# Seven gate columns of the input projection moved next to and into the scan's prologue turns, with the modulation rows and their products in a new fixed order

## The chip, the cores and the metric

The kernel runs on one core of a Trainium2 chip, as one launch. The metric is the device time of that launch in microseconds, lower is better. The names of the engines in the profile are PE (matrix products), DVE (vector), ACT (scalar, activations), POOL (GpSimd) and SP (which here only issues DMAs); PEld is PE's weight load. Everything is fp32: where an operand needs more than one PE pass carries, it is split into a high and a low half (`hh`, `hl` for tokens; `whi`, `wlo` for weights), and a product is three matmuls.

## The reference, cut to what matters

One layer of a diffusion backbone, with 256 context tokens and 2048 latent tokens of width 1024.

```python
mod_x = silu(c) @ w_ada + b_ada                  # six vectors of 1024: sh1, sc1, ga1, sh2, sc2, ga2
mod_c = silu(c_ctx) @ w_ada + b_ada              # the same for the context; sh and sc are used
hx = rmsnorm(x, norm1_g) * (1 + sc1) + sh1
px = hx @ w_in                                   # 15 x 128 RWKV columns | 512 Fourier | 2 x 1024 gates
qx = rwkv_inputs(centred_shift(px[..., :1920]))  # r, decays, keys, values, ...; the same for ctx
yx = bidir_wkv(qx, states left by the context)   # two recurrent scans over the tokens
fx = real(fftn(px[..., 1920:2432]))              # over the 32 x 64 grid and the group channels
x = x + ga1 * ((sigmoid(gate_f) * (fx @ w_up_f)
                + sigmoid(gate_r) * (group_norm(yx) * g @ w_up_r)) @ w_out)
x = x + ga2 * swiglu(rmsnorm(x, norm2_g) * (1 + sc2) + sh2)
```

## The kernel before

*Prologue.* The rows of `w_ada` come in tiles `wadar` (128 x 1024) and are multiplied on DVE with the broadcast silu vectors, `sB` of the latents (`mod_dve`, L130) and `sC` of the context (L151); the sum over the row is accumulated into `mod`. Eight tiles give sc1 for both; sh1 comes from eight tiles `wadak` on PE into `modps` (L157). The statistics of the norm are in `rs`. Then every 256 tokens `xs` go through `scaled` (L249: x times gain times rs), `moved` on ACT (L253: plus shift, rounded, `hh`) and on DVE (L254: the rest, `hl`), for each of the eight k slices of 128 channels.

*Input projection.* Three parts of 768 tokens (part 0 holds the context and 512 latents). Each part runs fifteen column turns. A turn loads one RWKV column of `w_in`, multiplies it (`pxps`), shifts and post-processes it (`z_stage`, `stack_z`, `k_norm`; `bnps` is the last matmul of a z stage, its result goes by `bsq` into DRAM `bv_dr`), and then does one or two of the twenty Fourier and gate columns, 15 to 34 (`gate_columns`, PSUM tile `fps`): a column of 768 tokens is 24 matmuls of 512 and 24 of 256 tokens. Parts 1 and 2 also load one `wada` row tile in a turn (32 in all, two in the last) for the modulation that later stages need, each with one product on DVE; all use one buffer. These stages are ordered by a list scheduler, except the instructions that are marked `keep_in_program_order`.

*Scan.* From L568 on everything is pinned: each engine executes in the order of the program (in the profile all such instructions have the line of the helper, L568). The scan has 18 blocks of 128 tokens in both directions, in turns s = -2 to 17. Turns -2 and -1 are the prologue turns, which prepare the blocks 0 and 1: `gram` (PE, `qk` from the loaded `BD` and `KR`), `masks` (DVE, `QK`), a store and reload (`AI`), `invert` (DVE, `tm` and `Q`), a store and reload (`TT`, `T`), `wps`, `t21ps`. A turn from 0 on has two chains in addition, which end in the state `ZC`: PE `xr`, `pu`, `pz`, ACT copies, DVE `ZC`. Between the steps stand seven calls of `fill()` in a turn, each of which takes one step of the generator `fourier()`: first the DFT over the grid (`hps` and `p`), then the product with `w_up_f` (stored to `fm_dr`), then the group norm of the first four token blocks (`gny`, `gnb`, `sg`, `s`). Before, 140 of its 141 steps are taken in the twenty turns.

*After the scan.* `c_merge` multiplies the normed blocks with `w_up_r` (`pr`), adds the gated Fourier part (`gr`, `gf`), `c_out` multiplies with `w_out`; then the feed-forward layer to the end.

Of the kernel before, what the change touches and what calls it, by code (L numbers as in the profile page):

```python
# [40 lines left out]
def layer_kernel(ctx: ExitStack, tc, I, out_T, dbg=None):  # L41
# [44 lines left out]
    pcT = pcs.enter_context(tc.tile_pool(name="pcp", bufs=1, side="right")).tile([128, TOT // C, 2, 4], F32, name="pcT", padded_shape=[128, 40, 2, 4])  # L86
    hpx = ctx.enter_context(ExitStack())
# [17 lines left out]
    def stats(xs, bank, eng=nc.vector, n=256):  # L105
        rs = hp.tile([128, 256], F32, tag="rs", name="rs", bufs=4)[:, 0:n]
        sq = hp.tile([128, KT, 256], F32, tag="sq", name="sq", bufs=1)[:, :, 0:n]
        nc.scalar.activation(out=sq, in_=xs, func=AF.Square)
        for m in (4, 2, 1):
            eng.tensor_tensor(out=sq[:, 0:m, :], in0=sq[:, 0:m, :], in1=sq[:, m:2 * m, :], op=ALU.add)  # L110
        ps = bank()[:, 0:n]
        nc.tensor.matmul(ps, ones, sq[:, 0, :], start=True, stop=True)
        rms_finish(rs, ps)
        return rs
# [12 lines left out]
    RS = [stats(xs, mm_bank, nc.gpsimd) for xs in XS]  # L127

    def mod_dve(w, s_, jt, j):
        nc.vector.scalar_tensor_tensor(out=w, in0=w, scalar=0.5, in1=s_, op0=ALU.mult, op1=ALU.mult, accum_out=mod[:, jt, j:j + 1])  # L130

    with tc.tile_pool(name="wa", bufs=1) as wa:
        th = wa.tile([128, 16], F32, name="th")
        nc.scalar.activation(out=th, in_=vec[:, V_C:V_C + 16], func=AF.Tanh, scale=0.5)
        sc2 = wa.tile([128, 16], F32, name="sc2")
        nc.vector.scalar_tensor_tensor(out=sc2, in0=th, scalar=1.0, in1=vec[:, V_C:V_C + 16], op0=ALU.add, op1=ALU.mult)
        sc3 = wa.tile([128, 8, 2], F32, name="sc3")
        nc.vector.tensor_scalar(out=sc3.rearrange("p k j -> p j k"), in0=sc2.rearrange("p (j k) -> p j k", j=2),
                                scalar1=0.5, scalar2=None, op0=ALU.mult)
        sC = wa.tile([128, D], F32, name="sC")  # L140
        nc.sync.dma_start(sC, I["cc"][1:2, :].to_broadcast([128, D]))
        tB = wa.tile([128, D], F32, name="tB")
# [3 lines left out]
        mps = pmm.tile([128, 512], F32, tag="mm", name="modps")  # L146
        for n in range(8):
            wr = wa.tile([128, D], F32, tag="wr", name=f"wadar{n}", bufs=3)
            nc.sync.dma_start(wr, I["w_ada"][8 + n])
            wj = wa.tile([128, D], F32, tag="wj", name=f"wadaj{n}", bufs=1)  # L150
            nc.vector.scalar_tensor_tensor(out=wj, in0=wr, scalar=0.5, in1=sC, op0=ALU.mult, op1=ALU.mult,  # L151
                                           accum_out=mod[:, 8 + n, 1:2])
            mod_dve(wr, sB, 8 + n, 0)
            wk = wa.tile([128, KT, 128], F32, tag="wk", name=f"wadak{n}", bufs=3)
            nc.sync.dma_start(wk, I["w_ada0"][n])
            for k in range(KT):
                nc.tensor.matmul(mps[:, 2 * n:2 * n + 2], wk[:, k, :], sc3[:, k, :], start=k == 0, stop=k == KT - 1)  # L157
# [3 lines left out]
        nc.vector.tensor_copy(mod[:, 0:8, :], mps[:, 0:16].rearrange("p (j c) -> p j c", c=2))
# [70 lines left out]


    carry = cst.tile([128, 15, 1], F32, name="carry")

    with ExitStack() as st:
# [9 lines left out]

        def scaled(k, xs, rs, j):
            x_ = xs[:, k, :]
            nc.vector.scalar_tensor_tensor(out=x_, in0=x_, scalar=gsc[:, k, j:j + 1], in1=rs, op0=ALU.mult, op1=ALU.mult)  # L249

        def moved(k, xs, j, hh, hl):
            x_ = xs[:, k, :]
            nc.scalar.activation(out=hh[:, k, :], in_=x_, func=AF.Identity, bias=mod[:, k, j:j + 1])  # L253
            nc.vector.scalar_tensor_tensor(out=hl[:, k, :], in0=x_, scalar=mod[:, k, j:j + 1], in1=hh[:, k, :].bitcast(F32),  # L254
                                           op0=ALU.add, op1=ALU.subtract)
# [131 lines left out]

        NP = 3
        for part in range(NP):
# [3 lines left out]
            cols = [(512, 256), (258, 0)] if part == 0 else [(512, p0), (258 if part < 2 else 256, p0 + 512)]  # L393
            H = [[hp.tile([128, KT, 512 - 248 * i], F32R, tag=f"h{y}{i}", name=f"h{y}{part}_{i}")[:, :, 0:n] for y in "hl"]
                 for i, (n, _) in enumerate(cols)]

            places = [(0, 0, 0), (0, 256, 0), (1, 0, 1 if part == 0 else 0)]
            for ps_ in (places[0:2], places[2:3]):
# [21 lines left out]
            for ci, ct in enumerate((12, 13, 0, 8, 4, 1, 9, 5, 2, 10, 6, 3, 11, 7, 14)):  # L420
                if part:
                    for jt in range(16 * part + ci, 16 * part + ci + 1 + (ci == 14)):
                        wr = hp.tile([128, D], F32, tag="sq", name=f"wada{jt}", bufs=1, padded_shape=[128, 2 * D])
                        tc.keep_in_program_order(nc.sync.dma_start(wr, I["w_ada"][jt]))
                        mod_dve(wr, sB, jt, 0)
# [54 lines left out]
                gate_columns((15 + ci, 30 + ci // 3) if ci % 3 == 2 else (15 + ci,), H, lats)  # L480
# [81 lines left out]
    class Pinned:  # L562
        def __init__(self, eng):
            self.eng = eng

        def __getattr__(self, name):
            f = getattr(self.eng, name)
            return lambda *a, **k: tc.keep_in_program_order(f(*a, **k))  # L568

    PE, DV, AC, GP, SY = [Pinned(x) for x in (nc.tensor, nc.vector, nc.scalar, nc.gpsimd, nc.sync)]  # L570

    with ExitStack() as st:
# [5 lines left out]

        ZC = sp.tile([128, 2, 4, 64], F32, name="ZC")
# [230 lines left out]
        def fourier():  # L810
            with tc.tile_pool(name="fd", bufs=1) as fd:
# [602 lines left out]
```

## Time and profile before

| | us |
|---|---|
| median of 3 runs | 3577.69 (3574.19 to 3580.49) |
| the profiled execution | 3574.86 |
| its span in the trace | 3573.1 |
| prologue to the first token matmul | 0 to 60 |
| input projection, three parts | 60 to 1053 |
| from its last matmul to the first of the scan | 1053 to 1066 |
| prologue turns | 1066 to 1135 |
| scan | 1135 to 1813 |
| to the first `pr` | 1813 to 1826 |
| merge, output, feed-forward | 1826 to 3573 |

The mean granted clock of PE is 0.952 of full speed, PE is busy in 91% of the span, DVE in 67%. In the rows of waits the figures are the total, the number of times, and the longest; a name behind `<-` in square brackets is what ended the idle time before the instruction. Rows of groups read: busy us, mean ns of one, idle time of the engine just before them.

### The profile page before, as it was taken

The numbers are of one execution on the slowest core, as the hardware profiler recorded it, in microseconds if no ns is written. First come the engines' busy times: TensorE is split into PE (matmuls) and PEld (weight loads), VectorE is DVE, ScalarE is ACT, GpSimd is POOL, SyncE is SP. The second block draws the span as 40 slices with busy tenths as digits, with TensorE's granted clock in tenths as the row PEclk, the third lists the DMA queues.
The fourth block names the chain that finished last, engine by engine and source line by source line (L and its number), as shares of the span: only waits on it lengthen the run. The fifth ranks groups of instructions, "written<-read, shape, count | busy, mean of one in ns | idle before, by whom it ended". The sixth has DMA issues, their size and how long they took to land.

```text
span 3573.1 us, 56290 instructions
## 1 busy us (share of the span) xinstructions
PE 3265.4 (91%) x20574; PEld 2696.8 (75%) x20574; DVE 2408.0 (67%) x4466; ACT 1553.2 (43%) x2908; POOL 697.1 (20%) x1099
## 2 busy tenths in 40 slices
PE   5999899999987888889769997999999999999987
PEld 5887788877875777777657776888877878888876
DVE  6577577746757776666568678777774387776354
ACT  3668557646643444344434235333353333333332
POOL 2142332222323332122132341000120000000000
PEclk9999999999997888999779999999999999999998
DMA  6254554545455567767467764222264332222442
GB/s 221 88 172 154 173 188 150 173 148 183 167 191 155 139 173 218 219 192 218 140 241 235 251 229 145 92 82 84 83 203 168 130 108 86 80 84 94 158 166 101
DMA packets 308436, 561.01 MB, mean 157 GB/s; under 512 B 91296, under 2 KB 102816, under 8 KB 308160
## 3 DMA queue, kind: packets, MB, share of 16 engines
q1 hardware_dynamic: 264256, 418.29, 36.1%
q0 software_dynamic: 43904, 139.12, 11.9%
q8 instruction: 163, 2.67, 0.3%
q14 instruction: 113, 0.93, 0.1%
HBM read 405.62 MB, written 151.66 MB: 156 GB/s over the span
## 4 chain that ended last, share of the span: by engine, by line
PE 28%; issue 12%; DVE 6%; DMA 3%; ACT 1%; POOL 1%; SPq 0%; DVEq 0%; POOLq 0%; ACTq 0%
PE pd L1267 12%; PE pT L199 2%; PE pT L200 2%; PE pT L201 2%; PE pB L199 2%; PE pB L200 2%; PE pB L201 2%; PE po L201 1%; PE po L199 1%; PE po L200 1%; DMA gr<-g_dr 1%; DVE wlo L193 1%; DMA wraw<-w_down 1%; DMA wA<-w_gu 1%; POOL u_dr L1215 1%
## 5 line engine op out<-in xcount | busy, mean ns | idle before, releaser
L193 DVE TENSOR_TENSOR wlo<-wraw,whi 128x512 fp32r<-128x512 f32 x472 | 318.5, 698 | 416.5 <-ACT whi L192 393.7
L192 ACT ACTIVATE whi<-wraw 128x512 fp32r<-128x512 f32 x472 | 283.3, 626 | 481.1 <-PE pd L1267 200.3
L1267 PE MATMUL pd<-uh,whi 128*128 128x512 f32 x704 | 278.5, 396 | 25.0 <-ACT whi L192 23.4
L199 PE MATMUL fps<-hh,whi 128*128 128x512 f32 (+1 forms) x800 | 285.9, 357 | 0.1
L201 PE MATMUL fps<-hh,wlo 128*128 128x512 f32 (+1 forms) x800 | 281.7, 352 | 0.1
L200 PE MATMUL fps<-hl,whi 128*128 128x512 f32 (+1 forms) x800 | 280.0, 350 | 0.0
L1267 PE MATMUL pd<-ul,whi 128*128 128x512 f32 x704 | 277.4, 394 | 0.0
L1267 PE MATMUL pd<-uh,wlo 128*128 128x512 f32 x704 | 254.6, 392 | 0.6 <-DVE wlo L193 0.6
L199 PE MATMUL pxps<-hh,whi 128*128 128x512 f32 (+2 forms) x720 | 248.8, 346 | 5.8 <-ACT hh L253 3.5
L200 PE MATMUL pxps<-hl,whi 128*128 128x512 f32 (+2 forms) x720 | 244.4, 341 | 4.7 <-DVE hl L254 4.7
L201 PE MATMUL pxps<-hh,wlo 128*128 128x512 f32 (+2 forms) x720 | 242.6, 342 | 0.5 <-DVE wlo L193 0.4
L1205 DVE TENSOR_TENSOR u<-u,pT 128x512 f32<-128x512 f32 x176 | 120.7, 686 | 142.6 <-PE pT L201 140.9
L1215 POOL DMA_DIRECT2D u_dr<-u x44 | 23.8, 541 | 842.3 <-DVE u L1214 811.1
L1267 PEld LDWEIGHTS pd<-uh,whi 128*128 128x128 f32 x704 | 134.1, 191 | 58.2 <-ACT whi L192 27.1
L568 DVE TENSOR_TENSOR tm<-Q,AI 128x126 f32<-128x126 f32 (+22 forms) x558 | 149.0, 267 | 42.9 <-DMA AI<-ab_dr 26.5
L199 PEld LDWEIGHTS fps<-hh,whi 128*128 128x128 f32 x800 | 150.8, 188 | 25.6 <-issue 4.3
L200 PEld LDWEIGHTS fps<-hl,whi 128*128 128x128 f32 x800 | 150.7, 188 | 24.2 <-issue 5.5
L201 PEld LDWEIGHTS fps<-hh,wlo 128*128 128x128 f32 x800 | 150.5, 188 | 23.4 <-issue 2.4
L568 DVE TENSOR_TENSOR Q<-Q,tm 128x126 f32<-128x126 f32 (+22 forms) x558 | 154.4, 277 | 20.2
L199 PEld LDWEIGHTS pxps<-hh,whi 128*128 128x128 f32 x720 | 136.5, 190 | 25.9 <-ACT hh L253 4.3
L1267 PEld LDWEIGHTS pd<-ul,whi 128*128 128x128 f32 x704 | 134.1, 191 | 27.9
L1267 PEld LDWEIGHTS pd<-uh,wlo 128*128 128x128 f32 x704 | 133.1, 189 | 29.2 <-DVE wlo L193 1.4
(715 smaller groups left out, 8550.3 us busy)
## 6 DMA issues: line engine op xcount, KB each, us to landing
wraw<-w_in SPq DMA_DIRECT2D x210, 256.0 KB, 3.1
wraw<-w_down SPq DMA_DIRECT2D x176, 256.0 KB, 2.9
wA<-w_gu SPq DMA_DIRECT2D x176, 256.0 KB, 2.6
BD<-bd_dr SPq DMA_DIRECT2D x36, 512.0 KB, 7.1
KR<-kr_dr SPq DMA_DIRECT2D x36, 512.0 KB, 8.1
wada<-w_ada SPq DMA_DIRECT2D x32, 512.0 KB, 4.5
wraw<-w_out SPq DMA_DIRECT2D x64, 256.0 KB, 3.2
wf<-wf_dr SPq DMA_DIRECT2D x32, 512.0 KB, 7.0
```

The source lines that it names most:

```text
L192: nc.scalar.activation(out=hi[:, k0:k1, :], in_=raw, func=AF.Copy)
L193: nc.vector.tensor_tensor(out=lo[:, k0:k1, :], in0=raw, in1=hi[:, k0:k1, :].bitcast(F32), op=ALU.subtract)
L199: nc.tensor.matmul(ps, wh[:, k, :], xh(k), start=start and k == 0, stop=False)
L200: nc.tensor.matmul(ps, wh[:, k, :], xl(k), start=False, stop=False)
L201: nc.tensor.matmul(ps, wl[:, k, :], xh(k), start=False, stop=stop and k == K - 1)
L568: return lambda *a, **k: tc.keep_in_program_order(f(*a, **k))
L1205: nc.vector.tensor_tensor(out=o, in0=x, in1=y, op=ALU.add)
L1215: nc.gpsimd.dma_start(u_dr[f][:, TT[hf]:TT[hf] + 512], c)
L1267: nc.tensor.matmul(PD[ct], x[:, ct, :], y, start=f == 0 and i == 0, stop=f == FT - 1 and i == 2)
```

## The change

Four things move.

1. *Prologue.* The products of the modulation, PE's `modps` matmuls, the ends of the statistics and the scaling of the first 512 latents are pinned, in this order: for each tile its `sB` product, and for the first five also its `sC` product; then per k slice and 256 tokens `xs`, `hh`, `hl`; the `sC` products of the last three tiles stand behind slices 3, 5 and 7.
2. *Modulation rows.* All 32 `wada` tiles are loaded in part 1, two or three in a turn, none in part 2.
3. *Gate columns.* Part 2 does only the columns 15 to 25 within its turns (RWKV column 7 comes last instead of 14), then 26 and 27, and then a new generator `late_gates()` does 28 to 34: nine of its steps (columns 28 to 30, tile `gps`) before the scan, the other twelve (31 to 34) in the fourteen `fill()` calls of turns -2 and -1. `fourier()` starts with turn 0. It has one step more than before, one extra call, and 127 calls within the scan; its last fifteen steps are taken behind the last turn.
4. *Memory.* The token halves live in a pool of their own until turn 0; then that room holds one of the three `QK` tags and one of the two `TT`. The tile `fo` of the gate columns has two buffers instead of three. The last addition of the statistics has its own tile `sm`.

```diff
+    hst = ctx.enter_context(ExitStack())
+    hh_ = hst.enter_context(tc.tile_pool(name="hh", bufs=1))
...
-            nc.vector.scalar_tensor_tensor(out=wj, in0=wr, scalar=0.5, in1=sC, op0=ALU.mult, op1=ALU.mult,
-                                           accum_out=mod[:, 8 + n, 1:2])
-            mod_dve(wr, sB, 8 + n, 0)
+            WR.append(wr)
+            w0 = wa.tile([128, D], F32, tag="w0", name=f"wada0{n}", bufs=1)
+            DV.scalar_tensor_tensor(out=w0, in0=wr, scalar=0.5, in1=sB, op0=ALU.mult, op1=ALU.mult, accum_out=mod[:, 8 + n, 0:1])
+            if n < 5:
+                mod_j1(n)
...
-                nc.tensor.matmul(mps[:, 2 * n:2 * n + 2], wk[:, k, :], sc3[:, k, :], start=k == 0, stop=k == KT - 1)
+                PE.matmul(mps[:, 2 * n:2 * n + 2], wk[:, k, :], sc3[:, k, :], start=k == 0, stop=k == KT - 1)
+            if n in (3, 6):
+                RS[n // 3 - 1] = RS[n // 3 - 1](PE, DV)
...
+        scale_of(0)
+        for k in range(KT):
+            for m in range(2):
+                scaled(k, XS[m], RS[m], 0, DV)
+                moved(k, XS[m], 0, *[x[:, :, 256 * m:256 * m + 256] for x in H0[0]], DV)
+            if k in (3, 5, 7):
+                mod_j1(5 + (k - 3) // 2)
+        scale_of(1)
...
-            for ci, ct in enumerate((12, 13, 0, 8, 4, 1, 9, 5, 2, 10, 6, 3, 11, 7, 14)):
-                if part:
-                    for jt in range(16 * part + ci, 16 * part + ci + 1 + (ci == 14)):
+            if part < 2:
+                gates = [(15 + ci, 30 + ci // 3) if ci % 3 == 2 else (15 + ci,) for ci in range(15)]
+            else:
+                n_ = iter(range(15, 26))
+                gates = [() if ci in (2, 6, 9, 14) else (next(n_),) for ci in range(15)]
+            for ci, ct in enumerate((12, 13, 0, 8, 4, 1, 9, 5, 2, 10, 6, 3, 11, 7, 14) if part < 2 else
+                                    (12, 13, 0, 8, 4, 1, 9, 5, 2, 10, 6, 3, 11, 14, 7)):
+                if part == 1:
+                    for jt in range(16 + 2 * ci + min(ci, 2), 18 + 2 * ci + min(ci + 1, 2)):
...
+        gate_columns((26, 27), H, lats, go_tile)
+        late = [load_w(I["w_in"][ct], KT) for ct in (28, 29)]
...
+    def late_gates():
+        cts = list(range(28, 35))
+        W_ = late
+        for i, ct in enumerate(cts):
+            for (hh, hl), (l0, n) in zip(H, lats):
+                ps = (pxr if i > 2 else pmm).tile([128, 512], F32, tag="xr" if i > 2 else "mm", name=f"gps{ct}_{l0}")
+                for h2 in range(2 if n == 512 else 1):
+                    ks = range(4 * h2, 4 * h2 + 4) if n == 512 else range(KT)
+                    for k in ks:
+                        for m, (a, x) in enumerate(((0, hh), (0, hl), (1, hh))):
+                            PE.matmul(ps[:, 0:n], W_[i][a][:, k, :], x[:, k, 0:n], start=k == 0 and m == 0, stop=k == KT - 1 and m == 2)
...
+                    yield
+
+    src = [late_gates()]
+    for _ in range(9):
+        next(src[0])
...
-        fo = fourier()
         def fill():
-            return next(fo, 0) is None
+            return next(src[0], 0) is None
...
         for s in range(-2, NS):
+            if s == 0:
+                while fill():
+                    pass
+                hst.close()
+                lt.append(st.enter_context(tc.tile_pool(name="lt", bufs=1, side="right")))
+                src[0] = fourier()
+                fill()
```

In the order of DVE's instructions, at the place of the first tokens, before (names are output and inputs; L249 is `scaled`, L254 `moved`, WL a weight half of a later product):

```order
L161 COPY mod<-modps 128x16
L162 TENSOR_TENSOR mod<-mod,vec 128x32
L167 SCALAR_TENSOR_TENSOR gsc<-mod,vec 128x8 x2
L249 SCALAR_TENSOR_TENSOR xs<-xs,gsc,rs 128x256 x15
L254 SCALAR_TENSOR_TENSOR hl_0_397<-xs,mod,hh_0_396 128x256 x3
L277 TENSOR_TENSOR WL_363<-wsraw,WS_0_367 64x512
```

and in the changed kernel, where pinned instructions have the line L59:

```order
L59 SCALAR_TENSOR_TENSOR wada_308,mod<-wadar_306,sB 128x1024
...
L59 TENSOR_TENSOR mod<-modps,vec 128x16
...
L59 SCALAR_TENSOR_TENSOR gsc<-mod,vec 128x8
...
L59 SCALAR_TENSOR_TENSOR xs<-xs,gsc,rs 128x256
L59 SCALAR_TENSOR_TENSOR hl_0_167<-xs,mod,hh_0_166 128x256
L59 SCALAR_TENSOR_TENSOR wadaj_349,mod<-wadar_273,sC 128x1024
```

The batch of fifteen scalings has become pairs of one `xs` and one `hl`, sixteen of them, with three `wadaj` products in between.

PE at the end of part 2, before (`fps` is a gate column, `hh_1` and `hl_1` are the halves of the 256-token piece, `qk` is the first product of the prologue turns):

```order
L199 MATMUL fps<-hh_1_6578,whi 128x256
L200 MATMUL fps<-hl_1_6579,whi 128x256
L201 MATMUL fps<-hh_1_6578,wlo 128x256
L371 MATMUL bnps<-bsq,cn 128x256
L568 MATMUL qk_0_0_0_9963<-KR_0_9949,BD_0_9947 128x128
```

and in the changed kernel (`gps` is a late gate column):

```order
L59 MATMUL gps_1792_9671<-hh_1_6649,wlo 128x256
L416 MATMUL bnps<-bsq,cn 128x256
L59 MATMUL gps_1792_9671<-hh_1_6649,whi 128x256
...
L59 MATMUL qk_0_0_0_9732<-KR_0_9718,BD_0_9716 128x128
...
L59 MATMUL gps_1280_9793<-hh_0_6647,whi 128x512
```

Behind the last `bnps` there now stand 18 matmuls of column 30, then the `qk` of turn -2, then column 31.

DVE behind the last step of the scan's chain, before:

```order
L568 TENSOR_TENSOR gny<-gny,s_18880 128x512
L568 TENSOR_TENSOR ZC<-pz_1_18996,ZC 128x512
L568 TENSOR_TENSOR ZC<-ZC,pcT 128x512
L568 TENSOR_TENSOR gnb<-gnb,gnv 128x512 x2
L205 TENSOR_TENSOR ol_19112<-gnb,oh_19111 128x4x128 x2
L568 TENSOR_TENSOR gnb<-gnb,gng 128x512
```

and in the changed kernel:

```order
L59 TENSOR_TENSOR ZC<-pz_1_18908,ZC 128x512
L59 TENSOR_TENSOR ZC<-ZC,pcT 128x512
L59 TENSOR_TENSOR gny<-gny,gnb 128x512
L59 TENSOR_REDUCE s_18973<-gny 128x8
L59 TENSOR_SCALAR s_18973<-s_18973 128x8
```

The group norm of the first four blocks, whose DVE rows stood ahead of the last `ZC` but for the last four, now begins behind it.

More of the change, by code (lines that the diff above doesn't have):

```diff
@@ L103, in load_x, with stats, finish @@
         return xs
-    def stats(xs, bank, eng=nc.vector, n=256):
-        rs = hp.tile([128, 256], F32, tag="rs", name="rs", bufs=4)[:, 0:n]
+    def stats(xs, bank, eng=nc.vector, n=256, later=False):
+        rs = hp.tile([128, n], F32, tag=f"rs{n}", name="rs", bufs=3 if n > 2 else 2)
         sq = hp.tile([128, KT, 256], F32, tag="sq", name="sq", bufs=1)[:, :, 0:n]
         nc.scalar.activation(out=sq, in_=xs, func=AF.Square)
-        for m in (4, 2, 1):
+        for m in (4, 2):
             eng.tensor_tensor(out=sq[:, 0:m, :], in0=sq[:, 0:m, :], in1=sq[:, m:2 * m, :], op=ALU.add)
[L111 to L114, printed above, removed]
+        sm = hp.tile([128, 256], F32, tag="sm", name="sm", bufs=1)[:, 0:n]
+        eng.tensor_tensor(out=sm, in0=sq[:, 0, :], in1=sq[:, 1, :], op=ALU.add)
+        def finish(pe=nc.tensor, dv=nc.vector):
+            ps = bank()[:, 0:n]
+            pe.matmul(ps, ones, sm, start=True, stop=True)
+            rms_finish(rs, ps, dv)
+            return rs
+        return finish if later else finish()
     def edge(c0, bank):
@@ L126, in layer_kernel, with scaled, moved, token_halves @@
     XS = [load_x(256), load_x(512)]
-    RS = [stats(xs, mm_bank, nc.gpsimd) for xs in XS]
-    def mod_dve(w, s_, jt, j):
-        nc.vector.scalar_tensor_tensor(out=w, in0=w, scalar=0.5, in1=s_, op0=ALU.mult, op1=ALU.mult, accum_out=mod[:, jt, j:j + 1])
+    RS = [stats(xs, mm_bank, nc.gpsimd, later=True) for xs in XS]
+    def scaled(k, xs, rs, j, dv=nc.vector):
+        x_ = xs[:, k, :]
+        dv.scalar_tensor_tensor(out=x_, in0=x_, scalar=gsc[:, k, j:j + 1], in1=rs, op0=ALU.mult, op1=ALU.mult)
+    def moved(k, xs, j, hh, hl, dv=nc.vector):
+        x_ = xs[:, k, :]
+        nc.scalar.activation(out=hh[:, k, :], in_=x_, func=AF.Identity, bias=mod[:, k, j:j + 1])
+        dv.scalar_tensor_tensor(out=hl[:, k, :], in0=x_, scalar=mod[:, k, j:j + 1], in1=hh[:, k, :].bitcast(F32),
+                                op0=ALU.add, op1=ALU.subtract)
+    def token_halves(part, cols):
+        return [[hh_.tile([128, KT, 512 - 248 * i], F32R, tag=f"h{y}{i}", name=f"h{y}{part}_{i}")[:, :, 0:n] for y in "hl"]
+                for i, (n, _) in enumerate(cols)]
+    COLS0 = [(512, 256), (258, 0)]
+    H0 = token_halves(0, COLS0)
+    gsc = cst.tile([128, 8, 2], F32, name="gsc")
+    def mod_dve(w, s_, jt, j, dv=nc.vector):
+        dv.scalar_tensor_tensor(out=w, in0=w, scalar=0.5, in1=s_, op0=ALU.mult, op1=ALU.mult, accum_out=mod[:, jt, j:j + 1])
     with tc.tile_pool(name="wa", bufs=1) as wa:
@@ L146, in layer_kernel, with mod_j1 @@
         mps = pmm.tile([128, 512], F32, tag="mm", name="modps")
+        WR = []
+        def mod_j1(n):
+            wj = wa.tile([128, D], F32, tag="wj", name=f"wadaj{n}", bufs=1)
+            DV.scalar_tensor_tensor(out=wj, in0=WR[n], scalar=0.5, in1=sC, op0=ALU.mult, op1=ALU.mult,
+                                    accum_out=mod[:, 8 + n, 1:2])
         for n in range(8):
@@ L245, in aux @@
             return ppx.tile([128, 512], F32, tag="aux", bufs=NAUX, name="rmsps")
[L247 to L255, printed above, removed]
         def edge_put(e, hh, hl):
@@ L391, in layer_kernel @@
             S = [px.tile([128, 768], F32R, tag=f"S{i}", name=f"S{part}_{i}", bufs=1) for i in range(4)]
[L393 to L395 removed]
+            cols = COLS0 if part == 0 else [(512, p0), (258 if part < 2 else 256, p0 + 512)]
+            H = token_halves(part, cols) if part else H0
             places = [(0, 0, 0), (0, 256, 0), (1, 0, 1 if part == 0 else 0)]
[L398 removed]
+            for ps_ in (places[0:2], places[2:3])[part == 0:]:
                 for k in range(KT):
@@ L826, in fourier @@
                     load_x(i)
+                yield
                 def adds(fv, q, j0, m):
```

65 lines of the change are left out of this document (41 added, 24 removed).

## The prediction

> **What bounds the kernel now.** I read the page's slices first, then the busy time by stage, then in each stage what the bounding engine waits for, and last single rows at the borders of the stages.
>
> ```profile
> PE   5999899999987888889769997999999999999987
> ...
> PEclk9999999999997888999779999999999999999998
> ```
>
> The slices are 89 us each. PE is full nearly everywhere, except in slice 0, in slices 12 to 19 (the scan and the two prologue turns ahead of it) and at 20; at the same places the granted clock falls. The windows below cut the span at those borders; the columns are length, busy time with count by engine, granted clock, DMA share, GB/s.
>
> ```profile
> 0.00:60.00 60.00, 30.82 (x136) 29.65 (x136) 37.28 (x66) 14.89 (x19) 14.63 (x27) 1.00 0.73 247
> 60.00:1053.00 993.00, 963.01 (x5030) 789.84 (x5030) 672.21 (x1147) 621.39 (x1127) 278.72 (x504) 1.00 0.48 160
> 1053.00:1066.00 13.00, 0.33 (x3) 0.03 (x1) 3.94 (x11) 1.05 (x2) 4.19 (x7) 0.62 0.60 216
> 1066.00:1135.00 69.00, 49.70 (x386) 41.26 (x387) 46.42 (x129) 17.76 (x38) 23.06 (x40) 0.70 0.53 156
> 1135.00:1813.00 678.00, 572.52 (x7858) 487.53 (x7858) 454.35 (x1311) 278.72 (x660) 168.57 (x300) 0.87 0.62 181
> 1813.00:1826.00 13.00, 6.97 (x55) 5.67 (x51) 5.97 (x10) 6.48 (x16) 3.61 (x4) 0.63 0.60 189
> 1826.00:1930.00 104.00, 83.14 (x350) 67.25 (x350) 91.21 (x144) 35.60 (x76) 46.99 (x33) 0.84 0.84 297
> 1930.00:3573.00 1643.00, 1558.95 (x6770) 1275.54 (x6770) 1096.60 (x1654) 577.32 (x972) 157.28 (x186) 0.98 0.39 132
> ```
>
> So the projection (row 2) is PE's: 963 of 993 us, at full clock. A matmul taken out of it is time taken out. The hole before the scan (row 3) is 13 us with PE empty. The prologue turns (row 4) and the scan (row 5) are chains of short steps over PE, DVE, ACT and DMA, with free PE time: 19 us and 105 us. After the last chain step (rows 6, 7) DVE is the fullest. The last row is untouched.
>
> **The sum** is made against the profiled execution, 3574.86 us, which is 2.8 under the median of 3577.69.
>
> **1. Prologue.** PE's two waits there, DVE's rows, and the prices:
>
> ```profile
> PE pxps L200 <- DVE hl L254: 4.2, 1, 4.2
> PE pxps L199 <- ACT hh L253: 2.2, 1, 2.2
> ...
> 58.33 0.17 DVE L161 COPY mod<-modps 128x16 f32<-128x16 f32 x1 [2.82 <-PE modps L157]
> ...
> 58.96 6.03 DVE L249 SCALAR_TENSOR_TENSOR xs<-xs,gsc,rs 128x256 f32<-128x256 f32 x15
> 64.91 1.27 DVE L254 SCALAR_TENSOR_TENSOR hl<-xs,mod,hh 128x256 fp32r<-128x256 f32 x3
> ```
>
> ```profile
> L151 DVE SCALAR_TENSOR_TENSOR wadaj<-wadar,sC 128x1024 f32<-128x1024 f32 x8 | 10.3, 1292 | 0.0
> ...
> L249 DVE SCALAR_TENSOR_TENSOR xs<-xs,gsc,rs 128x256 f32<-128x256 f32 x24 | 9.8, 480 | 0.0
> L254 DVE SCALAR_TENSOR_TENSOR hl<-xs,mod,hh 128x256 fp32r<-128x256 f32 x22 | 9.2, 477 | 0.1
> ...
> L253 ACT ACTIVATE hh<-xs,mod 128x256 fp32r<-128x256 f32 x24 | 10.2, 494 | 9.9 <-DVE xs L249 9.9
> ```
>
> Now modps is the last to come, at 58.33, after 2.82 us of waiting. Three products moved behind (3 x 1.29 = 3.9) and that wait away make 51.6 for the start of the scaling; DVE is busy 37.3 of the first 60 us, so with PE's order fixed it can be earlier still, and I estimate 48. But in the new order each hl stands directly behind its xs and waits for ACT: 480 + 494 + 477 ns, 1.45 us an item, x16 is 23.2, and three wadaj add 3.9: 27.1 from 48 is 75.1, against 58.96 plus 16 x 0.96 = 74.3 in the old batches. The last item, and the 258-token piece behind it, come hardly earlier; PE gets its first 512 tokens sooner, one slice in 3.4 us. Ends: -8 (PE fills both waits and more), +4 (the last piece is late). I take **-2**.
>
> **2. Thirty-two w_ada rows, all in part 1.** Where DVE waits now, and PE's longest wait in parts 1 and 2:
>
> ```profile
> DVE wada L130 <- DMA wada<-w_ada: 33.3, 16, 3.7
> ...
> PE fwp L222 <- ACT ft L220: 10.3, 11, 2.8
> ```
>
> DVE waits for these loads, PE does not show them. Twice the rate in part 1: with the 1.3 of a product and the 3.7 of the longest wait, two rows in a turn hold SP's queue for 2 x 5.0 = 10 us of a turn that lasts 22 (993 us for three parts of 15 turns), and the loads of w_in stand behind them. I take **+3** in part 1 (from 0, as PE shows nothing of it now, to +17, half of DVE's 33.3, if that much of the waiting reaches PE), nearer to 0 since a turn is twice as long as the two rows; and **-1** in part 2, which is free of them.
>
> **3. Columns out of the projection.** Columns 31 to 34 are now done in the prologue turns; 26 to 30 stay ahead of the qk.
>
> ```profile
> 1032.03:1043.09 11.06, 11.05 (x48) 8.83 (x48) 0.60 (x1) 1.00 0.34 121
> 1048.89:1052.40 3.51, 3.23 (x25) 3.02 (x25) 0.61 (x2) 1.00 0.64 219
> ```
>
> These windows hold gate matmuls alone: 0.230 us at 512 tokens, 0.129 at 256. A column is 24 x 0.230 + 24 x 0.129 = 8.62 us; four are **-34.5**.
>
> **4. The hole before the scan.**
>
> ```profile
> 1052.66 0.67 PE L371 MATMUL bnps<-bsq,cn 128*128 128x256 f32 x2 [0.54 <-ACT fo L212]
> ...
> 1055.53 0.72 POOL L306 DMA_DIRECT2D bv_dr<-bsq  x1 [0.28 <-DVE bsq L372]
> ...
> 1060.49 0.33 SPq L568 DMA_DIRECT2D BD<-bd_dr  x1
> ...
> 1066.00 0.59 PE L568 MATMUL qk<-KR,BD 64*128 64x128 f32 x2 [12.67 <-DMA BD<-bd_dr]
> ```
>
> bnps, bsq, its store, the load of BD, qk: 13.3 us in a row. The load still waits for that store, and in the new order only 18 matmuls of 256 (2.3 us) stand between bnps and qk. They fill, they don't shorten; column 14's stores, being earlier now, leave the queues freer. **-3** (0 to -12.7, the whole wait).
>
> **5. The prologue turns.** They lose the Fourier steps and get the four columns and three weight splits.
>
> ```profile
> 1066.00:1135.00 69.00, 8.40 (x38) 6.97 (x38) 3.15 (x6) 0.70 0.53 156
> 1066.00:1135.00 69.00, 8.28 (x24) 5.24 (x24) 2.85 (x6) 0.70 0.53 156
> ...
> DVE tm L568 <- DMA AI<-ab_dr: 10.9, 2, 10.5
> ...
> PE wps L568 <- DVE T L568: 5.5, 1, 5.5
> ...
> L193 DVE TENSOR_TENSOR wlo<-wraw,whi 128x512 fp32r<-128x512 f32 x472 | 318.5, 698 | 416.5 <-ACT whi L192 393.7
> ```
>
> The first two rows are the windows of tiles hps and p, Fourier's own: 16.7 of the 49.7 us of PE. What stays is 33.0; with 34.5 PE has 67.5 in 69 us. It just fits, because the chain's waits (10.5 for AI, 5.5 for T) are long enough to take a step of 12 matmuls (2.8 us). The splits are 6 x 0.70 = 4.2 us on DVE, which the AI wait covers if they come in it; gone with Fourier are its four loads ahead of AI on SP. If each of some six hand-overs is caught behind half a step, it is +8. Ends -4 and +14; I take **+4**.
>
> **6. The scan.** Fourier starts two turns later, with at least 14 of its steps not done at the end.
>
> ```profile
> 1139.55 0.68 DVE L568 TENSOR_TENSOR ZC<-pz,ZC 128x512 f32<-128x512 f32 x1
> ...
> 1717.44 0.68 DVE L568 TENSOR_TENSOR ZC<-pz,ZC 128x512 f32<-128x512 f32 x1
> ...
> 1763.42 0.68 DVE L568 TENSOR_TENSOR ZC<-pz,ZC 128x512 f32<-128x512 f32 x1
> ```
>
> Fifteen turns take (1717.44 - 1139.55)/15 = 38.5 us each, the sixteenth 46.0: there the group norm's first row waits 9.6 us on DVE for sg (the row below), with the chain queued behind it. That row now stands behind the last chain step. **-8** (-14 to 0).
>
> **7. After the scan.**
>
> ```profile
> L568 DVE TENSOR_TENSOR gny<-gny,gnb 128x512 f32<-128x512 f32 x4 | 2.7, 685 | 9.6 <-DMA sg<-sg_dr 9.6
> ...
> L568 DVE TENSOR_TENSOR gnb<-gnb,gnv 128x512 f32<-128x512 f32 x2 | 1.4, 692 | 8.9 <-ACT gnb L568 8.9
> L568 DVE TENSOR_TENSOR gnb<-gnb,gng 128x512 f32<-128x512 f32 x2 | 1.4, 688 | 6.0 <-PE gng L568 6.0
> ...
> 1717.44:1813.00 95.56, 13.01 (x28) 0.82 (x4) 0.68 0.36 103
> ```
>
> The last row is the window of tile s, which covers the norm's other rows: 13.0 + 2.7 + 1.4 + 1.4 = 18.5 us of DVE work that four blocks did inside the scan before 1813, free. Now it opens a stretch in which DVE is busy 97 of 117 us. Packed at that density it is 22; the pinned rows' own waits (8.9 + 6.0 above) make it up to 33; nothing, if all went into the 20 us that DVE idles there. The rows stand in front of the first pr, so the top half is likelier: **+25**.
>
> Sum: -2 + 3 - 1 - 34.5 - 3 + 4 - 8 + 25 = **-16.5**, so 3558.4 against the profile and 3561.2 against the median. I say 3559.
>
> **Rivals.**
> (a) The tail is hidden: the group norm's late rows fit into DVE's 20 idle us. For: PE and DVE together leave room in rows 6 and 7. Against: 88% DVE there, and pr needs all four blocks. 3559 - 25 = 3534.
> (b) Slower: the late columns stand in front of the chain. PE takes its queue in order, and four columns at the stage's clock of 0.70 are 34.5/0.70 = 49 us. If nothing of it fits into waits, the turns grow by 49 rather than 4: 3604. It decides from 20 us on. Against: 19 us of free PE time and 16.7 of Fourier's.
> (c) No change: in part 1 PE runs dry behind the wada bursts. At 1.3 us a turn the 15 turns cost 20, not 3, and eat the sum: 3576. For: SP's order; against: not one PE wait there names a load.
> (d) The clock. Stage 4 ran at 0.70 beside broken PE work, the projection at 1.00. If the dense columns hold it up, the 33.0 us of the turns' own matmuls shrink by up to 0.3 x 33 = 10: 3549. [...]
>
> **Chances.** Forecast 0.53 (3546 to 3570), (a) 0.15, (b) 0.12, (c) 0.10, (d) 0.10. For 8 in 10, the range takes in (a), (c), (d) and the forecast's own spread, 3533 to 3582, and leaves out (b) and the far ends of several steps at once. About 0.2%, 7 us, can be told from no change: faster is the forecast, (a) and (d), 0.78; same is (c), 0.10; slower (b), 0.12.
>
> **What would show it.** Step 1: first pxps near 48 and hl rows 1.4 us apart. Step 2: PE waits for whi in 350 to 715. Step 3: qk at about 1066 - 38 = 1028. Step 4: a wait of 9 to 11 before qk. Step 5: first ZC 72 to 78 us after qk, and few waits of PE for AI's chain; over 95 is (b). Step 6: no turn over 42 us. Step 7: first pr 35 us or more after the last ZC, where it was 13; under 20 is (a). The forecast is wrong above all if 5 or 7 is mis-sized, since they are the terms with the widest ends.

## The result, and the profile after

The changed kernel is slower: 3584.84 us against 3573.97 (medians of 20 runs each), a ratio of 1.0032 with a 95% interval of 1.0021 to 1.0044. One of the changed kernel's twenty runs was slow (5369 us at a granted clock of 0.555) and is not in the ratio. The profiled execution has a span of 3581.5 us, 8.4 over the one of before.

The page's slices of PE and of its clock, after:

```profile
PE   6999899999988887998758898999998999999997
...
PEclk9999999999999887999869998999999999999998
```

Against before, the dent at the prologue turns (slice 12) is shallower in both rows, and the one at slice 20, behind the scan, is deeper (before: PE 6 and clock 7 there, now 5 and 6). By stage (length, busy time with count by engine, clock, DMA share, GB/s), with the borders at the first token matmul, the first matmuls of parts 1 and 2, the first `qk`, the first and the last `ZC` of a chain, and the first `pr`:

```profile
0.00:56.00 56.00, 31.09 (x136) 29.55 (x136) 36.19 (x62) 15.32 (x19) 13.79 (x14) 1.00 0.76 263
56.00:357.00 301.00, 288.41 (x1343) 226.48 (x1343) 216.81 (x382) 204.32 (x370) 79.71 (x157) 0.97 0.43 137
357.00:722.00 365.00, 346.68 (x1847) 286.10 (x1848) 263.19 (x447) 222.59 (x394) 118.09 (x183) 0.99 0.56 187
722.00:1043.70 321.70, 308.19 (x1652) 255.03 (x1651) 195.43 (x329) 193.23 (x355) 87.96 (x175) 0.98 0.46 152
1043.70:1123.50 79.80, 70.13 (x594) 61.26 (x594) 51.17 (x148) 19.00 (x40) 18.77 (x37) 0.90 0.51 152
1123.50:1773.50 650.00, 571.32 (x7817) 484.52 (x7816) 436.23 (x1262) 277.34 (x654) 177.56 (x312) 0.89 0.64 185
1773.50:1830.00 56.50, 15.94 (x89) 13.08 (x86) 32.63 (x62) 16.93 (x41) 13.50 (x10) 0.53 0.75 249
1830.00:3581.00 1751.00, 1640.08 (x7111) 1344.22 (x7109) 1173.35 (x1781) 611.57 (x1042) 191.97 (x212) 0.96 0.42 138
```

The same marks in all the traces, as lengths of the stretches in us:

| kernel | to first token matmul | part 0 | part 1 | part 2 to qk | qk to first ZC | scan | last ZC to pr | pr to end | span |
|---|---|---|---|---|---|---|---|---|---|
| before | 60.4 | 291.5 | 354.4 | 359.6 | 73.6 | 673.3 | 13.1 | 1747.1 | 3573.1 |
| after | 56.2 | 300.7 | 364.8 | 321.9 | 79.9 | 650.0 | 56.6 | 1751.4 | 3581.5 |
| k1_fills | 56.3 | 299.7 | 362.8 | 323.1 | 80.0 | 706.5 | 9.1 | 1742.7 | 3580.2 |
| k2_wada | 56.3 | 300.0 | 362.4 | 318.9 | 80.1 | 640.2 | 58.9 | 1747.4 | 3564.1 |
| k3_prol | 60.9 | 287.8 | 365.0 | 322.6 | 81.1 | 647.2 | 55.6 | 1751.7 | 3571.9 |
| k4_all | 61.7 | 287.5 | 359.6 | 317.9 | 79.4 | 702.7 | 11.3 | 1742.5 | 3562.6 |
| k5_early | 55.6 | 302.0 | 362.4 | 321.5 | 80.1 | 712.2 | 10.3 | 1741.4 | 3585.5 |
| k6_early_all | 61.2 | 287.5 | 363.1 | 318.4 | 80.1 | 702.7 | 11.1 | 1742.9 | 3566.8 |
| k7_hole_all | 59.7 | 287.5 | 358.8 | 355.2 | 70.3 | 670.5 | 12.5 | 1741.3 | 3555.7 |
| k8_bef_wada | 60.8 | 291.8 | 367.6 | 364.4 | 75.0 | 667.5 | 12.7 | 1746.4 | 3586.0 |
| k9_bef_fo2 | 61.7 | 291.7 | 357.3 | 359.5 | 74.0 | 670.8 | 12.4 | 1743.6 | 3571.1 |
| k11_bef_nofill | 59.0 | 293.1 | 358.1 | 360.1 | 72.5 | 644.1 | 57.4 | 1749.6 | 3593.8 |
| k12_hole3 | 61.3 | 287.4 | 359.0 | 349.6 | 69.4 | 662.1 | 13.0 | 1744.1 | 3546.0 |

From before to after: the first token matmul is 4.2 us earlier, but part 1 begins 4.9 later; part 1 is 10.4 longer; part 2 with the hole 37.7 shorter; the prologue turns 6.3 longer; the scan 23.3 shorter; the tail 43.5 longer and what follows 4.3 longer. That adds up to the 8.4. Single traces of one kernel differ by some us in a stage (k11 and before have the same projection: 3.7 apart in part 1), so the verdicts below go by the timed runs, 6 to 12 of each version, and the stages tell where. A ratio is always to the kernel before, timed alongside. The changed kernel was not timed again, so the difference of a version to it is a difference of two ratios, each good to 0.001 to 0.002, 4 to 7 us.

### The profile page after: what moved, and what is told of

It reads as the page before. It is cut to its first block, busy times and chain, and to the rows that moved or that the text cites. A ratio compares the mean times of both kernels' runs of the same rounds, so it can differ in the third digit from the quotient of the medians.

```text
span 3581.5 us, 56320 instructions
## 1 busy us (share of the span) xinstructions
PE 3271.8 (91%) x20574; PEld 2700.2 (75%) x20574; DVE 2405.0 (67%) x4467; ACT 1560.3 (44%) x2910; POOL 701.3 (20%) x1099
## 4 chain that ended last, share of the span: by engine, by line
PE 36%; issue 10%; DVE 6%; DMA 6%; ACT 1%; POOL 1%; SPq 0%; DVEq 0%; POOLq 0%; ACTq 0%
PE pd L1352 12%; PE pT L251 2%; PE pT L252 2%; PE pT L253 2%; PE pf L59 2%; PE pB L251 2%; PE pB L252 2%; PE pB L253 2%; PE po L253 1%; PE po L251 1%; PE po L252 1%; PE xr L59 1%; DMA gr<-g_dr 1%; PE qk L59 1%; DMA wraw<-w_down 1%
## 5 line engine op out<-in xcount | busy, mean ns | idle before, releaser
L245 DVE TENSOR_TENSOR wlo<-wraw,whi 128x512 fp32r<-128x512 f32 x462 | 310.0, 695 | 378.3 <-ACT whi L244 365.6
L251 PE MATMUL fps<-hh,whi 128*128 128x512 f32 (+1 forms) x688 | 249.2, 362 | 0.1
L253 PE MATMUL fps<-hh,wlo 128*128 128x512 f32 (+1 forms) x688 | 245.6, 357 | 1.4 <-DVE wlo L245 1.4
L252 PE MATMUL fps<-hl,whi 128*128 128x512 f32 (+1 forms) x688 | 243.6, 354 | 0.0
L59 DVE TENSOR_TENSOR tm<-Q,AI 128x126 f32<-128x126 f32 (+22 forms) x558 | 150.2, 269 | 29.5 <-DMA AI<-ab_dr 12.9
L59 DVE TENSOR_TENSOR Q<-Q,tm 128x126 f32<-128x126 f32 (+22 forms) x558 | 154.7, 277 | 20.2
L252 PEld LDWEIGHTS pxps<-hl,whi 128*128 128x128 f32 x720 | 138.2, 192 | 20.6 <-issue 3.4
L253 PEld LDWEIGHTS pxps<-hh,wlo 128*128 128x128 f32 x720 | 138.0, 192 | 20.5 <-DVE wlo L245 3.8
L253 PEld LDWEIGHTS fps<-hh,wlo 128*128 128x128 f32 x688 | 130.4, 190 | 24.0 <-DVE wlo L245 3.0
```

The costliest lines, as they stand in the source:

```text
L245: nc.vector.tensor_tensor(out=lo[:, k0:k1, :], in0=raw, in1=hi[:, k0:k1, :].bitcast(F32), op=ALU.subtract)
L251: nc.tensor.matmul(ps, wh[:, k, :], xh(k), start=start and k == 0, stop=False)
L252: nc.tensor.matmul(ps, wh[:, k, :], xl(k), start=False, stop=False)
L253: nc.tensor.matmul(ps, wl[:, k, :], xh(k), start=False, stop=stop and k == K - 1)
```

## The experiments

**1. Fourier back into the scan: k1_fills.**

```diff
             at(h2, turn_b, s + 2, 1, 1)
+            if 0 <= s < 15:
+                fill()
```

> The changed kernel with one more fill() in each of the turns 0 to 14, so that the Fourier generator ends inside the scan again, as it did before the change. Theory T1 (the group norm of the first four blocks moved behind the last chain step costs more there, 43.5 us to the first pr, than the 20.9 us that turns 15 to 17 win by its going): 22 to 27 us faster than the changed kernel, near 3560, first pr 13 to 17 us behind the last ZC, turn 15 again near 46 us. Rival R1 (the scan is as long as its fills; fifteen extra steps lengthen the turns by as much as the tail wins): no change, near 3582, turns 0 to 14 about 1.6 us longer each.

Measured 1.0012 of before (0.9999 to 1.0025), against the changed kernel's 1.0032. The two intervals just overlap. The tail is gone (9.1 us), but the scan is 56.5 us longer, and the trace's sum is the same. R1 is the nearer one, though not in its place: the turns 0 to 7 stay as they were, the later ones go from 38 to 45 us. PE's waits there (turns 8 to 15; total, times, longest), first k1, then the changed kernel:

```profile
PE pf L59 <- DMA wf<-wf_dr: 28.7, 6, 7.5
PE pf L59 <- DMA fh<-fth_dr: 10.9, 3, 4.1
```

```profile
PE pf L59 <- DMA wf<-wf_dr: 11.0, 3, 4.4
```

The eighth step of a turn asks for a weight that the once-a-turn prefetch has not brought. So this run doesn't tell whether the steps cost so much anywhere.

**2. Modulation rows in both parts: k2_wada.**

```diff
-                if part == 1:
-                    for jt in range(16 + 2 * ci + min(ci, 2), 18 + 2 * ci + min(ci + 1, 2)):
+                if part:
+                    for jt in range(16 * part + ci, 16 * part + ci + 1 + (ci == 14)):
```

> The changed kernel with the 32 modulation rows spread over parts 1 and 2 again, one in a turn. Theory T2 (the second and third row in a turn hold SP and DVE, and PE's short waits in part 1 and the half clock behind them come from that): part 1 (the 720th to the 1440th pxps matmul) falls from 364.9 to about 355, part 2 rises by about 1, in all 7 to 10 us faster than the changed kernel. Rival R2 (the waits come from the two buffers of fo or from where the scheduler put the evictions): part 1 stays at 362 to 366, no change.

1.0010 (0.9993 to 1.0028): some 8 us off the changed kernel by the ratios, as T2 says, but the intervals overlap, and part 1 has only gone from 364.8 to 362.4, which lies in R2's range. So this run alone shows neither the gain nor its place. Run k8, below, does the same part alone.

**3. The prologue not pinned: k3_prol.**

```diff
-            if n < 5:
+            if n < 8:
                 mod_j1(n)
...
-                scaled(k, XS[m], RS[m], 0, DV)
+                scaled(k, XS[m], RS[m], 0)
```

(and so for the other pinned DVE and PE instructions there; the three products behind the slices go.)

> The changed kernel with the prologue's products, statistics and scaling not pinned, and all eight sC products next to their sB products. Theory T3 (the pinned pairs of xs and hl feed PE one slice in 2.9 us or more, its idle gaps keep it at half clock up to 85 us, and so the earlier start is lost by 90 us and more by 350): part 1 starts 4 to 8 us earlier than in the changed kernel, where it starts at 356.9, though the first token matmul comes later than 56.2. Rival R3 (the pinned order is good and part 0 is late for another reason, such as the smaller fo): part 1 starts at 356 to 362.

1.0017 (1.0001 to 1.0032). T3 holds: the first token matmul is at 60.9, 4.7 us later than in the changed kernel, and part 1 begins at 348.7, 8.2 us earlier than there and 3.3 earlier than before. The same 40 us, from 56 to 96, of k3 and of the changed kernel (the first figure behind the length is PE's busy time with its matmuls, the third from the end the clock):

```profile
56.00:96.00 40.00, 30.51 (x138) 24.59 (x139) 31.30 (x72) 26.88 (x54) 4.51 (x10) 1.00 0.41 133
```

```profile
56.00:96.00 40.00, 31.32 (x114) 22.19 (x115) 29.13 (x64) 19.35 (x37) 4.85 (x19) 0.83 0.32 92
...
PE pxps L251 <- ACT hh L152: 9.3, 6, 2.9
```

PE does 24 matmuls fewer in the same busy time, at a clock of 0.83: the pinned pairs of `xs` and `hl` feed it a slice at a time, and it waits six times for `hh`, five of them between slices (6.5 us). The clock of 1.00 in k3's row flatters it: from 66.85 to 72 us its matmuls, too, start 0.43 us apart, and 0.23 from there on. All five versions without the pins have 287.4 to 287.8 us in part 0, the four with them 299.7 to 302.0. Which of the pinned groups costs it was not taken apart further.

**4. The three together: k4_all.**

> The three edits together, so that of the change the moved columns and the memory plan remain. By T1, T2 and T3 the gains add: 33 to 42 us faster than the changed kernel, 22 to 31 us faster than before, near 3546. By the rivals one or more of the gains is missing.

1.0005 (0.9990 to 1.0021), near 0.27% below the changed kernel, not 1%. The two gains of 2 and 3 are there, the third is not: the scan is 702.7 us, as in k1.

**5. Fourier's extra steps in the early turns: k5_early and k6_early_all.**

```diff
             at(h1, load_v, s + 1, 1)
             fill()
+            if 0 <= s < 7:
+                fill()
...
             at(h2, turn_b, s + 2, 1, 1)
+            if 0 <= s < 8:
+                fill()
```

k6 has the edits of 2 and 3 besides.

> The changed kernel with the fifteen extra fill() calls in the early turns, two more in each of 0 to 6 and one in 7, where Fourier's steps are the small ones of the grid DFT, not the ones that wait for loads of w_up_f. Theory T1 (the tail behind the scan costs more than the late turns win; what made the first version of this give nothing were the extra steps in turns 8 to 14, whose weights came late): the turns 0 to 7 keep 37 to 39 us, the scan is 670 to 678 us, the first pr 9 to 14 us behind the last ZC, 18 to 28 us faster than the changed kernel. Rival R1 (turns are as long as their fills, early ones too): turns 0 to 6 are 3 to 6 us longer each, and the result is within 8 us of the changed kernel.

> The same with the modulation rows in parts 1 and 2, one in a turn, and the prologue not pinned. By T1: 3545 to 3552, 0.6 to 0.8% faster than before. By R1: no faster than the earlier version of these three edits, 1.0005 of before.

k5 is 1.0030 (1.0018 to 1.0043), the changed kernel's time: R1. The early half of the scan (first ZC to the 16th chain's, 15 chains) is longer by 34 us, the tail shorter by 46, and the later turns, now fuller of the `pf` steps, 28 longer. k6 is 0.9982 (0.9969 to 0.9995), so at last faster than before, by some 6 us, far from T1's 0.6%. What it has over k5, some 17 us, is what 2 and 3 bring together. The early half in k5 and in the changed kernel, and the longest wait in k5:

```profile
1121.60:1431.70 310.10, 252.65 (x3329) 220.52 (x3327) 203.89 (x580) 125.37 (x291) 103.10 (x177) 0.81 0.60 172
...
DVE T L59 <- DMA TT<-tb_dr: 35.3, 9, 21.5
```

```profile
1123.50:1399.60 276.10, 234.88 (x3280) 206.56 (x3278) 207.77 (x579) 121.55 (x284) 101.21 (x176) 0.86 0.58 163
```

The time of the turns is not PE's work alone (17.8 us more). It is also no even price of a step: of the 35 us by which the turns 0 to 6 are longer, turn 4 has 12.5 and turn 6 has 17.6 (k6: the same two). In turn 6 the product with `w_up_f` begins, a turn earlier than in the changed kernel, and its loads `fh`, `fl` and `wf` stand on SP ahead of the chain's own `TT`:

```profile
1391.32 0.32 SPq L59 DMA_DIRECT2D fl<-ftl_dr  x1
1392.66 3.99 SPq L59 DMA_DIRECT2D TT<-tb_dr  x4
...
1399.19 1.43 DVE L59 STREAM_TRANSPOSE T<-TT 32x512 f32<-32x512 f32 x2 [21.46 <-DMA TT<-tb_dr]
```

T1, in which the tail was dear and the scan had room, is false for these places too; that a longer chain link as such would cost this is not shown. What stays is a new theory, T6: the fifteen steps of Fourier cost 1.6 to 2.0 us each in the mean in the places tried, and were free where they stood.

**6. That displacement alone: k11_bef_nofill.** The kernel before, in which `fill()` does nothing in turns -2 and -1.

```diff
         def fill():
-            return next(fo, 0) is None
+            return False if idle[0] else next(fo, 0) is None
...
+            idle[0] = s < 0
```

> The kernel before with the fourteen Fourier steps taken out of turns -2 and -1, so that Fourier starts with turn 0 and ends behind the scan, as in the changed kernel; no column is moved into their place. Theory T6 (these steps were all but free in the prologue turns, and cost 1.6 to 2.0 us each wherever else they stand, so that the moved columns pay for their place what they win): from the first ZC to the end 20 to 30 us longer than before's 2433.5, first pr 50 to 58 us behind the last ZC, prologue turns (first qk to first ZC) 64 to 73 us against 73.6; 12 to 25 us slower than before. Rival R6 (the prologue turns were held up by these steps as much): they shrink to under 60 us, and the time stays within 7 us of before.

1.0085 (1.0064 to 1.0106), 30 us slower, with no column moved. The prologue turns are 72.5 us without their Fourier steps, against 73.6 with: free there, as T6 says. Behind, the scan and the tail come out as in the changed kernel:

```profile
1142.70:1786.80 644.10, 567.52 (x7815) 481.87 (x7815) 433.81 (x1261) 277.23 (x654) 177.26 (x311) 0.90 0.64 186
1786.80:1844.00 57.20, 15.92 (x91) 13.06 (x88) 32.64 (x62) 16.85 (x40) 13.26 (x10) 0.53 0.73 246
```

From the first ZC to the end it is 2451.1 us, 17.6 over before, a little under the 20 that T6 asked for; the timed runs say 30, more than its 12 to 25. Before's one trace is at the high end there: k8 and k9, which are the same program from the scan on, have 2426.5 and 2426.8. Over the mean of the three, 2428.9, k11 is 22.2 us longer.

**7. The rows of `w_ada` in part 1 alone: k8_bef_wada.** The kernel before, with the changed kernel's two lines of experiment 2.

> The kernel before with the 32 modulation rows all in part 1, two or three in a turn, and nothing else changed. Theory T2 (these rows cost PE's waits in part 1): part 1 goes from 354.4 to 359 or more, part 2 falls by 1 to 2, 3 to 6 us slower than before. Rival R2 (part 1 got slower in the changed kernel by the smaller fo, the clock or the scheduler's order): part 1 within 2 us, no change.

1.0054 (1.0034 to 1.0074): 19 us, three times T2's figure and more. Part 1 is 367.6, 13.2 longer, and part 2, which has none of these loads, is 4.8 longer too, which T2 doesn't explain. PE's waits in part 1 for the weights of `w_in` that come late are larger; the first row is before's, which has none for `wlo`, the other two are k8's:

```profile
PE pxps L199 <- ACT whi L192: 1.2, 2, 0.6
```

```profile
PE pxps L199 <- ACT whi L192: 6.0, 3, 4.1
...
PE pxps L201 <- DVE wlo L193: 1.8, 2, 1.4
```

In the changed kernel the same move costs less. In part 1 the four versions with all rows there (the changed kernel, k1, k3, k5) have 362.4 to 365.0 us, the five with the rows spread 358.8 to 363.1: 3 us in the mean. From part 2 to `qk` the same four have 321.5 to 323.1, against 317.9 to 318.9 of k2, k4 and k6, which have the same columns: 4 us, in the part that has none of the loads.

**8. Two buffers of fo: k9_bef_fo2.** The kernel before with `bufs=2` in `fo_tile`.

> The kernel before with two buffers of fo instead of three. Theory T5 (what makes part 1 of the changed kernel some 6 us longer than before's 354.4, with the modulation rows spread as before, is the missing buffer): part 1 at 358 to 362, all three parts 8 to 15 us longer in sum, 0.2 to 0.4% slower. Rival R5 (the buffer is worth nothing; the 6 us are half-clock periods of PE behind short waits, which come in one run and not in another): part 1 within 3 us, no change of the time.

1.0000 (0.9986 to 1.0015): the buffer is worth nothing that these runs can tell. Part 1 is 357.3 there, and 358.1 in k11, both with before's own columns, so 354.4 is at the low end of one program's spread. The five versions with the rows spread and the changed kernel's memory plan have 358.8 to 363.1, 4 us more in the mean; that rest stays unexplained. So T5 is out.

**9. The columns in the hole: k7_hole_all and k12_hole3.** The edits of 2 and 3, and the columns 31 to 34 ahead of the prologue turns, behind the issue of the first loads; Fourier starts with turn -2 as before. In k12 column 31 stands ahead of that issue.

```diff
+        for _ in range(3):      # k12 only
+            fill()
         load(0)
         load(1)
+        while fill():
+            pass
+        hst.close()
+        lt.append(st.enter_context(tc.tile_pool(name="lt", bufs=1, side="right")))
+        src[0] = fourier()
+        fill()
         gram(0, 0, 0)
...
-            if s == 0:
-                while fill():
-                    pass
...
```

> The change without its third part's core: the columns 31 to 34 run ahead of the prologue turns, behind the issue of the first loads of BD, so that they fill the hole there, and Fourier starts with turn -2 as before; modulation rows in both parts, prologue not pinned. Theory T4 (what a late column is worth beyond the hole is what the prologue turns can take; the hole itself takes up to 12 us): qk waits for nothing, the stretch from the 1440th pxps matmul to the first ZC is 8 to 13 us shorter than before's 433, the scan and the first pr are as before, in all 5 to 12 us faster than before. Rival R4 (the loads of BD come later by as much, or the columns there run at half clock): the stretch is within 4 us of before's, no change.

> The version with columns 31 to 34 in the hole ahead of the prologue turns, with the three steps of column 31 (and so the loads of the weights of column 32) put ahead of the issue of the first loads of BD. Theory T7 (PE's last wait there, 8.0 us before column 32, is for weights whose loads stood behind 4 MB of BD and KR on SP): that wait falls under 3 us, the stretch from the 1440th pxps matmul to the first ZC goes from 425.5 to 417 to 421, 4 to 8 us faster than that version, 0.9935 to 0.9950 of before. Rival R7 (the wait is for the eviction of column 31, as its row says, or BD is now late by as much): the wait or one of 5 us or more before qk stays, no change to that version.

k7 is 0.9959 (0.9945 to 0.9973), so R4 is out; its stretch from part 2's first matmul to the first ZC is 7.7 us shorter than before's, just under T4's 8, and part 0's 4 us come on top. qk waits for nothing any more, but a new wait stands before column 32; in k12 it is a third:

```profile
PE gps L59 <- ACT go L59: 8.0, 1, 8.0
```

```profile
PE gps L59 <- ACT go L59: 2.7, 1, 2.7
```

So T7 holds: not the eviction that the row names, but the loads behind BD on SP. ACT's row in k7 says the same of the weights of column 32:

```profile
1032.55 1.26 ACT L59 ACTIVATE whi<-wraw 128x512 fp32r<-128x512 f32 x2 [14.07 <-DMA wraw<-w_in]
```

k12 is 0.9949 (0.9931 to 0.9966), 18 us faster than before, the best of the versions; its stretch from part 2's first matmul to the first ZC is 419.0 us, against 433.2 before. That it beats k7 is what the medians say (3551.4 beside 3570.2 of the kernel before, and 3557.3 beside 3572.8); the intervals of the two ratios overlap.

## Why the prediction was wrong

The forecast was -16.5 us and the trace has +8.4. Steps 1, 2 and 6 with 7 make nearly all of the 25:

- **Step 1, -2, measured +4.9 at the start of part 1.** The pairs of `xs` and `hl` came 1.46 us apart, as the step said. Two things failed. The start was mis-sized: the scaling began at 52.6 and not at the estimated 48, so the last of the sixteen `hl` ended at 79.3 and not at 75.1. Without the pins (k3) it begins only 1.6 us later and the last `hl` ends at 71.7, since the batches don't wait for ACT (13 of the changed kernel's sixteen `hl` idle 0.57 or 0.58 us for `hh`). And the overlap with PE was left out: fed one slice in 2.9 or 4.1 us, PE idles between (6.5 us), and a mean clock of 0.83 over 40 us is what a third of them at half speed makes (from 72.5 to 78.5 the clock reads 0.50, and matmuls of 512 tokens start 0.43 us apart; from 87.6 on it reads 1.00, and they start 0.23 apart). The upper end, +4, was near; the value taken was not.
- **Step 2, +3 in part 1 and -1 in part 2, measured +10.4 in part 1.** Not all of that is the rows. By the versions of experiment 7 their price in the changed kernel is 3 us in part 1, which is the step's own figure, and 4 in part 2, where the step had a gain of 1. Some 4 of the 10.4 are in the versions with the rows spread as well and are unexplained, and the rest is the spread of single traces, before's low 354.4 above all. In the kernel before the same move costs 19 us (k8). So the failed step is that PE would be free again in part 2 and that loads of `w_in` behind `wada` stay hidden: "PE shows nothing of it now" was right of one row in a turn, and was carried to two. Nor could PE's rows have named a load, as rival (c) was answered: weights that come late show as waits for ACT's `whi` (6.0 us in part 1 of k8). Rival (c) had the direction and, in the kernel before, the size. Why part 2 pays is not shown in full; in the changed kernel it opens behind a wait of 2.6 us for `whi` with a clock of 0.83 in 10 us.
- **Steps 3 and 4, -34.5 and -3, with part 2's -1 together -38.5, measured -37.7.** The price of a column held. The sum is right in part by luck: part 2 lost the 4 of step 2, and the rest won as much more than was forecast (k2, k4 and k6, with the rows spread, are 40.7 to 41.7 shorter than before). Some of that is the wait before qk, which was 7.3, shorter than the 9 to 11 expected. qk came at 1043.7 and not at 1028, since the start of part 1 and part 1 itself had lost 15.
- **Step 5, +4, measured +6.3.** Right in size, so rival (b) is false. The clock did rise, from 0.72 to 0.90 between the first qk and the first ZC, and the turns did not get shorter, so rival (d) is false: PE's speed did not set them. The 10.5 us for AI, which step 5 counts as room for the columns, are a wait of DVE, and PE did Fourier's steps in them from 1076.3 on; PE's own longest waits in the stage were 5.5 and 4.4. k11 shows the same from the other side: with 15 us less of PE work than before the turns are as long, and PE waits in one piece for DVE. The first row is before's, the other two are k11's:

```profile
1066.00:1139.60 73.60, 54.07 (x458) 44.85 (x458) 50.57 (x143) 19.84 (x41) 26.62 (x49) 0.72 0.51 148
```

```profile
1070.20:1142.70 72.50, 38.84 (x402) 33.77 (x402) 47.28 (x143) 11.85 (x26) 14.29 (x29) 0.67 0.44 126
...
PE qk L568 <- DVE QK L568: 16.1, 1, 16.1
```

- **Steps 6 and 7, -8 and +25, together +17, measured -23.3 and +47.8, together +24.5.** Each was wrong by about a factor of two or more, and the two errors cancel for the most part: the sum is nearer than the mechanism. The scan won 23.3 instead of 8, since not the stall alone went but all of the group norm's rows: the sixteenth and the seventeenth turn are 10 us shorter each. The tail lost 43.5 + 4.3 instead of 25. The failed step is that it took the tail as DVE work at DVE's density. It is a chain of latencies instead:

```profile
1773.06 0.32 SPq L59 DMA_DIRECT2D fm_dr<-ev  x1
1777.98 0.33 SPq L609 DMA_DIRECT2D g<-g  x1
1778.37 0.42 SPq L59 DMA_DIRECT2D gny<-y_dr  x1
...
1783.45 0.69 DVE L59 TENSOR_TENSOR gny<-gny,gnb 128x512 f32<-128x512 f32 x1 [8.55 <-DMA gny<-y_dr]
...
PE gnt L59 <- DMA gf<-g_dr: 17.0, 1, 17.0
PE gnt L59 <- DVE gny L59: 13.4, 1, 13.4
```

The first load of the norm is issued only when the last store of Fourier has landed (`gn_open` takes the room of Fourier's tiles), 4.5 us behind the last ZC; DVE idles 8.6 us, and PE does 16 us of work in the 56.5. In the scan the same loads had been hidden behind the turns, but for 9.6 us of waiting for `sg`. No run issues them earlier, so what of the tail they make is not shown. The step's ends, 0 and 33, were too narrow, because both were counted in DVE time.

The prediction did price what the columns drive out, with those +17, but on DVE's time alone. k11 measures it by itself: 30 us in the timed runs and 22 in its trace from the first ZC on, for the fourteen steps alone; k1 and k5 tried two other places in the scan, and neither brought the 18 to 27 us that were expected of it. In the trace of the change the columns win 38, pay 6 for their new place and 24 for the steps that they drive out. The 7 that are left are less than the 15 that the prologue and part 1 lose. The version with the rows spread, the prologue not pinned and the tail left as it is was not run, so whether the columns alone win anything in that place stays open.

## What to carry to other kernels

Idle time that is already filled with other work is not free: before moving work into it, price what it drives out in the place where that will stand, by taking it out alone (here three changed lines, and 30 us). A hole with nothing in it is another thing: the same columns put ahead of the prologue turns, where PE had nothing to do, shortened that stretch by 14 us (k12), and with the prologue not pinned the kernel was 0.5% faster. When two terms come out of one shift, as the scan's gain and the tail's loss here, check each against its own stage: a sum that is nearly right can hide two that are not. And a pinned order that lets the first item start earlier can lose it again when it hands the items over one by one.

## What the runs showed of the hardware

Short waits of PE in a dense stream were at times followed by a stretch at half clock (a reading of 0.50), and at times not. The 10 us from such a wait on (2.7 us in the changed kernel, 2.8 in the kernel before; the clock is the third figure from the end):

```profile
400.00:410.00 10.00, 9.31 (x47) 7.49 (x46) 5.33 (x10) 3.77 (x7) 1.84 (x3) 0.83 0.70 229
```

```profile
416.40:426.40 10.00, 9.38 (x50) 7.71 (x50) 1.81 (x4) 1.89 (x4) 1.81 (x3) 1.00 0.20 52
```

The 0.83 is 3.4 us at half speed: from 401.3 to 404.7 the clock reads 0.50 and matmuls of 256 tokens start 0.21 us apart, and behind that it reads 1.00 and they start 0.12 apart. That costs 1.7 on top of the wait. The clock's row does not catch every such stretch: behind a wait of 4.17 us at 65.8 the kernel before starts matmuls of 512 tokens 0.43 us apart until 69.4 and 0.23 apart from 69.8 on, and the clock of 65.8 to 69.4 reads 1.00. Behind the wait of 2.8 us it starts them 0.23 apart from 417.5 on. What decides between the two is not shown. Such stretches may be part of why part 1 of one program takes 354 us in one trace and 358 in another: PE is busy for 342.35 us of it in the kernel before and for 345.39 in k11, with a matmul less.
